# Hybrid encoder trunk on one core: two products of the last FFN's block scheme change places, a step of one unit stands between two of them, and the final sums are spread over three steps

## The chip, the cores and the metric

The kernel runs on one core of a Trainium2 chip. Its time is the device time of one execution in microseconds, from the first to the last instruction and what lies around it; the figure for a kernel is the median of its timed runs.

## The reference

A trunk of two layers (`DEPTH = 2`) over 512 tokens of width 1024. Layer 0 mixes tokens with a gated short convolution, layer 1 with a chunked state-space mixer. Behind each mixer stands a SwiGLU feed-forward network of hidden width 2816. The change is in the second matrix product of the last of these, and in what follows it to the output.

```python
def swiglu_ffn(h, w_in, w_out):
    gate, up = jnp.split(h @ w_in, 2, axis=-1)
    return (jax.nn.silu(gate) * up) @ w_out

# in the loop over layers
        h = rmsnorm(x, norm_g[i, 2]) * (1.0 + scale) + shift
        y = swiglu_ffn(h, f_w_in[i], f_w_out[i])
        x = x + gate * rmsnorm(y, norm_g[i, 3])
    return x
```

Everything is float32. The tensor engine multiplies operands that are split into a high and a low part, so that each product of two tiles is three matmuls (high by high, low by high, high by low).

## The kernel before, in words

**The block scheme.** The last product, `y = hidden @ w2`, has 512 tokens, 2816 hidden values and 1024 columns. The hidden values are taken in pairs of blocks of 128: 11 pairs, numbered p = 0 to 10 (`NP`). Tokens are halved (256 and 256), columns are halved (512 and 512), and the two blocks of a pair are the halves in the third direction. So each pair is a 2 by 2 by 2 block product, done with seven products instead of eight (Strassen's scheme in Winograd's form). The tuple `PRODUCTS` lists the seven: the accumulator that a product adds into (`A`, `B`, `C`, `D`), the weight block (`b11`, `b12`, `b21`, `b22`) and the activation block (`a11`, `a12`, `a21`, `a22`, `s1`). The blocks are overwritten in place with sums as the scheme goes on:

- `t1`: `b12 += b11`, and `t2_`: `b22 += b12`, and `t4`: `b21 += b22`. These are accumulating DMAs, issued on GpSimd's queue (POOL) by `add_`.
- `t3`: `b11 = b22 - b11`, on VectorE (DVE).

In the kernel before, the order is: A with `b11`, B with `b21`, C with `b22` as loaded, A with `b22` after `t2_`, D with `b12` after `t1`, A with `b11` after `t3`, A with `b21` after `t4`. A is one running sum: it is read in between (after its first, second, third product and at the end), while it goes on adding. Each accumulator is two PSUM banks, one for each 128 of the 256 tokens (`t` or `sub` is 0 or 1).

**Units and steps.** The weights of the 11 pairs lie in 9 storage units: pairs (0,1), (2,3), then each of 4 to 10 alone (`units`, `unit_of`). Seven products of 11 pairs are 77 turns; `turns[i]` gives the order of the pairs in product i. Two turns make a step, 39 steps in all (`NT`), the last with one turn. Where a product ends on an odd turn, a step holds the last turn of one product and the first of the next. A step of two turns is 12 matmuls: for `sub` 0, then for `sub` 1, three for each turn (`products`, one recorded line, L1787). The last three steps are run together: `sub` 0 of all three, then `sub` 1.

**Preparation.** `w_prep(n)` splits the weights of step n: ScalarE (ACT) copies the high part (L1752), DVE subtracts for the low part (L1753). `a_prep(n)` does the same for the activations (L1765 and L1766). The split weights have 4 buffers, the split activations 3. So `w_prep(n + 4)` and `a_prep(n + 3)` wait until the tensor engine is through step n.

**The order of the engines' work is written out by hand.** This stretch is under a manual schedule for TensorE, ACT, DVE, POOL and SyncE's queue (SP): each engine takes its instructions in the order in which the code issues them. For each step n the loop issues `products([n])`, then `behind(n)`, then `w_prep(n + 4)`, then `a_prep(n + 3)`; from n = 34 `behind(n)` comes last. `behind(n)` holds what is tied to a step: `t3`, `t2_`, `t4`, and the evacuation of the accumulators into the four quarters of the result (`got["11"]`, `"12"`, `"22"`; the fourth is read from the bank itself), then the sum of squares (`square`, `mean`), the root (`root`), the gate (`gated`, L1991) and the residual with the output's DMA (`x_new`, L1997). L2037 is the subtraction of A from `got["22"]` at n = 32, L2019 that of A from `got["12"]` at n = 21, L2021 the addition of D at n = 27.

SP loads the blocks of `w2` in the order of the `w2_load` calls (L1574); POOL's accumulating DMAs (L1626) wait for those loads and for the splits that still need the old contents.

Of the kernel before, what the change touches and what calls it, by code (L numbers as in the profile page):

```python
# [18 lines left out]
D = 1024  # L19
# [12 lines left out]
MUL, ADD, SUB = ALU.mult, ALU.add, ALU.subtract  # L32
# [3 lines left out]
def trunk_kernel(  # L36
# [9 lines left out]
    act, dve, pe, pool = nc.scalar, nc.vector, nc.tensor, nc.gpsimd  # L46
# [523 lines left out]
    with ExitStack() as ph:  # L570
# [112 lines left out]
        with tc.manual_schedule(engines={PE_ENGINE, mybir.EngineType.SP, mybir.EngineType.Activation,  # L683
# [199 lines left out]
            for p in range(2):  # L883
# [13 lines left out]
            parts = out_begin(0, w_out0, lambda k: acts[k], KD, ggs, xn_tile, "aux", None,  # L897
                              ffn_after(0), ada_tile)
            for k in range(18):
                i, jp = k % 6, 2 + k // 6 * 2  # L900
# [98 lines left out]
        with tc.manual_schedule(engines={PE_ENGINE, mybir.EngineType.SP, mybir.EngineType.Activation,  # L999
# [3 lines left out]
            for i, f in ((0, 0), (2, 0), (1, 1), (3, 1), (4, 2), (5, 3)):  # L1003
# [5 lines left out]
                else:  # L1009
                    gate(f, lead_ps[i])  # L1010
                sums(1)
            parts = out_begin(1, f_w_out[0], lambda k: acts[k], NF, ggs, xn_tile, "aux", ssd_lead,
                              lambda: load_w([(wm_in, P, P)]))
            tiles = []
            for k in range(2 * NF - 6):
# [8 lines left out]
                q, j = divmod(k - 3, 4)  # L1024
# [25 lines left out]
    with ExitStack() as ph:  # L1050
# [299 lines left out]
        def xn_half():  # L1350
            return yp.tile([P, T], F32, tag="y", name="xn")

        parts = out_begin(2, wm_out, y_act, 16, gg2, lambda: (xn_half(), xn_half()), "mm",
                          all_of(ffn_lead(1, tile4b)), ffn_after(1))
# [169 lines left out]
        with tc.manual_schedule(engines={PE_ENGINE}):  # L1524
# [11 lines left out]

    PRODUCTS = (("A", "b11", "a11"), ("B", "b21", "a12"), ("C", "b22", "a12"), ("A", "b22", "a11"),
                ("D", "b12", "s1"), ("A", "b11", "a21"), ("A", "b21", "a22"))  # L1540

    with ExitStack() as ph:
        fo = ph.enter_context(tc.tile_pool(name="fo", bufs=3, reuse_waits="tile"))
# [3 lines left out]
        NP = NF // 2  # L1547
# [5 lines left out]
        units = [(0, 1), (2, 3)] + [(p,) for p in range(4, NP)]  # L1553
# [179 lines left out]

        even = list(range(NP))
        odd = [4, 0, 1, 2, 3] + list(range(5, NP))
        turns = [odd if i % 2 else even for i in range(7)]
        turns[2] = [4, 5, 0, 1, 2, 3] + list(range(6, NP))
        steps = [(i, p) for i in range(7) for p in turns[i]]
        NT = (len(steps) + 1) // 2
        w_of, a_of = {}, {}  # L1740

        def w_prep(n):
            w = whl_p.tile([P, 2, 2, T], F32R, tag="whl", name="whlo")
            part = steps[2 * n:2 * n + 2]
            us = {unit_of[p] for _, p in part}
            if len(us) == 1 and len(part) == 2:
                todo = [(slice(0, 2), b_(us.pop(), PRODUCTS[part[0][0]][1]))]
            else:
                todo = [(slice(q, q + 1), b_(unit_of[p], PRODUCTS[i][1])[:, units[unit_of[p]].index(p):][:, :1])
                        for q, (i, p) in enumerate(part)]  # L1750
            for sl, srcw in todo:
                act.copy(w[:, 0, sl, :], srcw)  # L1752
                dve.tensor_tensor(w[:, 1, sl, :], srcw, w[:, 0, sl, :].bitcast(F32), SUB)  # L1753
            w_of[n] = w

        def a_prep(n):
            a = fo.tile([P, 2, 2, 256], F32R, tag="ao", name="ao")
            part = steps[2 * n:2 * n + 2]
            if len(part) == 2 and part[0][0] == part[1][0] and part[1][1] == part[0][1] + 1:
                todo = [(slice(0, 2), part[0], 2)]  # L1760
            else:
                todo = [(slice(q, q + 1), st, 1) for q, st in enumerate(part)]
            for sl, (i, p), m in todo:
                srca = a_(PRODUCTS[i][2], p, m)
                act.copy(a[:, 0, sl, :], srca)  # L1765
                dve.tensor_tensor(a[:, 1, sl, :], srca, a[:, 0, sl, :].bitcast(F32), SUB)  # L1766
            for _, (i, p), m in todo:
                if i == 0:
                    dve.tensor_tensor(a_("a11", p, m), a_("s1", p, m), a_("a11", p, m), SUB)
                elif i == 1:  # L1770
                    dve.tensor_add(a_("a12", p, m), a_("a12", p, m), a_("a11", p, m))
            a_of[n] = a

        bank = {}

        def products(tiles):
            for sub in range(2):
                for n in tiles:
                    for q, (i, p) in enumerate(steps[2 * n:2 * n + 2]):
                        r = PRODUCTS[i][0]  # L1780
                        if r not in bank:
                            bank[r] = [(mm_ps if r == "C" else aux_ps)(f"c{r}{t}") for t in range(2)]
                        first = i == {"A": 0, "B": 1, "C": 2, "D": 4}[r] and p == turns[i][0]
                        last = p == turns[i][-1]
                        w, a, tk = w_of[n], a_of[n], slice(sub * P, (sub + 1) * P)
                        for k, (hl, al) in enumerate(((0, 0), (1, 0), (0, 1))):
                            pe.matmul(bank[r][sub], a[:, al, q, tk], w[:, hl, q, :],  # L1787
                                      start=first and k == 0, stop=last and k == 2, skip_group_check=True)

        with tc.manual_schedule(engines={PE_ENGINE, mybir.EngineType.SP, mybir.EngineType.Activation,  # L1790
# [5 lines left out]
            def t3(p):  # L1796
                i = unit_of[p]
                q = units[i].index(p)
                dve.tensor_tensor(b_(i, "b11", q), b_(i, "b22", q), b_(i, "b11", q), SUB)

            def t2_(i):
                add_(b_(i, "b22"), b_(i, "b12"))

            def t4(i):
                add_(b_(i, "b21"), b_(i, "b22"))
# [113 lines left out]
            u = UN - 1  # L1919
# [39 lines left out]
            late = range(5, len(units))  # L1959
# [3 lines left out]
            w2_load(4, "b21")  # L1963
            for i in late:
                w2_load(i, "b21")
            for i in (3, 1, 4, *late):
                w2_load(i, "b22", "b12")
            for n in (2, 3):
                w_prep(n)
            a_prep(2)  # L1970
            for i in (2, 3, 0, 1, *range(4, len(units))):
                t1(i)

            st = [{"s2": small(2), "s1": small(1), "b1": small(1)} for _ in range(4)]
# [3 lines left out]
            got = {}  # L1978
# [11 lines left out]
            def gated(src, hf, dst):  # L1990
                dve.tensor_mul(dst, src, gg[hf])  # L1991
                return dst

            def x_new(t, hf, yg, parts=(FULL,), puts=(dma,)):
                for c, put in zip(parts, puts):
                    cx = slice(hf * T + c.start, hf * T + c.stop)
                    dve.scalar_tensor_tensor(xt[t][:, cx], yg[:, c], st[t]["s1"], xt[t][:, cx], MUL, ADD)  # L1997
                    put(out[0, t * P:(t + 1) * P, cx], xt[t][:, cx])

            def behind(n):  # L2000

                if 14 <= n < 14 + NP:
                    t3(turns[5][n - 14])
                for i in (2, 3, 0, 1, *range(4, len(units))):
                    if n == 8 + turns[2].index(units[i][-1]) // 2:
                        t2_(i)
                    if n == 15 + i:
                        t4(i)
                for t in range(2):
                    if n == 5:  # L2010
                        got["11", t] = t2("c11")
                        act.copy(got["11", t], bank["A"][t])
                    elif n == 10:
                        dve.tensor_add(got["11", t], got["11", t], bank["B"][t])
                    elif n == 16:
                        got["12", t] = t2("c12")
                        act.copy(got["12", t], bank["C"][t])
                    elif n == 21:
                        dve.tensor_tensor(got["12", t], got["12", t], bank["A"][t], SUB)  # L2019
                    elif n == 27:  # L2020
                        dve.tensor_add(got["12", t], got["12", t], bank["D"][t])  # L2021
                        got["22", t] = spare[f"c22_{t}"]
                        act.copy(got["22", t], bank["D"][t])
                    elif n in (29, 30):
                        if t == n - 29:
                            square(t, 0, got["11", t])
                            square(t, 1, got["12", t])
                            mean(t)
                    elif n == 31:
                        root(t)  # L2030
                        gated(got["11", t], 0, got["11", t])
                        gated(got["12", t], 1, got["12", t])
                    elif n == 33:
                        x_new(t, 0, got["11", t])
                        x_new(t, 1, got["12", t])
                    elif n == 32:
                        dve.tensor_tensor(got["22", t], got["22", t], bank["A"][t], SUB)  # L2037
                    elif n == 34:
                        square(2 + t, 0, got["22", t])
                        mean(2 + t)  # L2040
                    elif n == 35:
                        gated(got["22", t], 1, got["22", t])

            for n in range(NT - 3):
                products([n])
# [5 lines left out]
                if n + 4 < NT:  # L2051
                    w_prep(n + 4)
                if n + 3 < NT:
                    a_prep(n + 3)
# [42 lines left out]
```

## Time and profile before

| | us |
|---|---|
| median of three runs | 1351.39 (1349.91 to 1351.97) |
| the profiled execution's own time | 1351.48 |
| its span, first to last instruction | 1349.2 |
| TensorE busy in the span | 1329.8 (99%) |
| VectorE busy | 984.9 (73%) |
| ScalarE busy | 618.2 (46%) |
| first matmul of the changed product, from the span's start | 1226.38 |

The profile is of one execution. Times in its views are counted from the start of the span. PE is TensorE's matmuls, PEld its weight loads, DVE VectorE, ACT ScalarE, POOL GpSimd, SP SyncE. A row of the timeline is: start, length, engine, line, operation, tiles written and read, shape, count, and in brackets how long the engine was idle before it and what ended that. Matmuls overlap, so a row's length runs some 0.16 us past the start of what follows it. PEclk is the share of the full clock that TensorE was granted.

### The profile page before, as it was taken

To read this page: it belongs to the slowest core of one execution; us is meant where nothing else is said; L and a number is where in the kernel's file an instruction comes from. 1 tells how busy PE (TensorE), PEld (TensorE's weight loads), DVE (VectorE), ACT (ScalarE), POOL (GpSimd) and SP (SyncE) were. 2 spreads that over 40 slices of the span, in tenths; PEclk is the share of its full clock that TensorE was granted. 3 is DMA by queue.
4 is the path that set the end of the run, shared out by engine and by line. 5 is a ranking of instruction groups with operands and counts; after the bars stand their busy time and mean duration, and the time that the engine had idled before them with its cause. 6 is when DMAs were issued, how large, how long until landed. Compare 5 with 4: busy or idle time off the path is not lost.

```text
span 1349.2 us, 19124 instructions
## 1 busy us (share of the span) xinstructions
PE 1329.8 (99%) x7485; PEld 1145.6 (85%) x7485; DVE 984.9 (73%) x1581; ACT 618.2 (46%) x995; POOL 65.1 (5%) x82
## 2 busy tenths in 40 slices
PE   8999999999999999999999999999999999999896
PEld 6788889888888888898888888888899999998685
DVE  5588866778777322668988988887678777758696
ACT  5323355222322212655554555554474555545564
POOL 0000000000000000000000000000000111200420
PEclk9999999999999999999999999999999999999998
DMA  9757760777776322414534243413342888868851
GB/s 307 237 180 230 253 203 1 233 249 233 236 250 203 125 94 91 132 33 144 157 110 138 80 127 110 140 65 123 113 122 61 219 198 213 215 198 268 142 105 63
DMA packets 199886, 215.90 MB, mean 160 GB/s; under 512 B 8292, under 2 KB 148468, under 8 KB 198772
## 3 DMA queue, kind: packets, MB, share of 16 engines
q1 hardware_dynamic: 186384, 184.74, 44.1%
q0 software_dynamic: 9264, 17.04, 7.3%
q10 hardware_dynamic: 4148, 12.90, 3.1%
q8 instruction: 59, 0.97, 0.3%
q14 instruction: 31, 0.25, 0.1%
HBM read 195.37 MB, written 2.24 MB: 146 GB/s over the span
## 4 chain that ended last, share of the span: by engine, by line
PE 89%; DMA 4%; DVE 2%; ACT 2%; issue 2%; SPq 1%; POOL 1%; DVEq 0%; POOLq 0%; ACTq 0%
PE ip L276 14%; PE ip L278 14%; PE ip L277 14%; PE sA L1694 6%; PE y L378 6%; PE y L379 6%; PE y L380 6%; PE sC L1694 3%; PE cA L1787 2%; PE li L276 2%; PE li L278 2%; PE li L277 2%; PE li L756 2%; PE sB L1694 1%; PE yd L1283 1%
## 5 line engine op out<-in xcount | busy, mean ns | idle before, releaser
L276 PE MATMUL ip<-h,whl 128*128 128x512 f32 x840 | 331.2, 394 | 0.2 <-DVE cv L863 0.2
L278 PE MATMUL ip<-h,whl 128*128 128x512 f32 x840 | 327.2, 390 | 0.0
L277 PE MATMUL ip<-h,whl 128*128 128x512 f32 x840 | 327.0, 389 | 0.0
L276 PEld LDWEIGHTS ip<-h,whl 128*128 128x128 f32 x840 | 157.7, 188 | 33.9 <-issue 1.8
L278 PEld LDWEIGHTS ip<-h,whl 128*128 128x128 f32 x840 | 157.6, 188 | 33.2
L277 PEld LDWEIGHTS ip<-h,whl 128*128 128x128 f32 x840 | 157.8, 188 | 31.8
L222 DVE TENSOR_TENSOR whl<-wst,whl 128x1024 fp32r<-128x1024 f32 x99 | 120.4, 1221 | 60.6 <-ACT whl L221 60.4
L124 DVE SCALAR_TENSOR_TENSOR ada_acc<-ada_st,csil,ada_acc 128x512 f32<-128x512 f32 x140 | 105.0, 750 | 3.9 <-DMA ada_st<-in_ada_w_dram 0.4
L204 DVE TENSOR_TENSOR whlo<-wsto,whlo 128x1024 fp32r<-128x1024 f32 x41 | 49.9, 1224 | 78.1 <-ACT whlo L203 78.0
L221 ACT CAST whl<-wst 128x1024 fp32r<-128x1024 f32 x99 | 103.0, 1041 | 4.3 <-DMA wst<-in_a_w_in_dram 2.2
L276 PE MATMUL li<-h,whl 128*128 128x256 f32 x288 | 83.2, 289 | 0.0
L278 PE MATMUL li<-h,whl 128*128 128x256 f32 x288 | 81.6, 283 | 0.0
L277 PE MATMUL li<-h,whl 128*128 128x256 f32 x288 | 81.5, 283 | 0.0
L203 ACT CAST whlo<-wsto 128x1024 fp32r<-128x1024 f32 x41 | 42.6, 1050 | 76.3 <-PE y L380 71.1
L1694 PE MATMUL sA<-tq,whl 128*128 128x256 f32 x576 | 74.6, 283 | 0.3 <-DVE g L1720 0.3
L1694 PEld LDWEIGHTS sA<-tq,whl 128*128 128x128 f32 x576 | 71.6, 192 | 0.6 <-DVE g L1720 0.5
L1787 PE MATMUL cA<-whlo,ao 128*128 128x512 f32 x264 | 64.3, 402 | 6.0 <-DVE w2h L2037 3.7
L378 PE MATMUL y<-whlo,ff 128*128 128x512 f32 x176 | 68.6, 390 | 0.0
L380 PE MATMUL y<-whlo,ff 128*128 128x512 f32 x176 | 68.5, 389 | 0.0
L379 PE MATMUL y<-whlo,ff 128*128 128x512 f32 x176 | 68.5, 389 | 0.0
L1787 PEld LDWEIGHTS cA<-whlo,ao 128*128 128x128 f32 x264 | 51.3, 195 | 18.0 <-issue 4.1
L1142 DVE SCALAR_TENSOR_TENSOR cu<-ip,cols,cu 128x511 f32<-128x511 f32 (+2 forms) x84 | 62.8, 748 | 3.9 <-ACT cu L1139 1.4
(328 smaller groups left out, 2436.9 us busy)
## 6 DMA issues: line engine op xcount, KB each, us to landing
ada_st<-in_ada_w_dram SPq DMA_DIRECT2D x96, 512.0 KB, 5.3
wst<-in_f_w_in_dram SPq DMA_DIRECT2D x26, 1024.0 KB, 6.5
wst<-in_m_w_in_dram SPq DMA_DIRECT2D x14, 1024.0 KB, 5.4
wsto<-in_f_w_out_dram SPq DMA_DIRECT2D x10, 1024.0 KB, 5.0
wst<-in_m_w_in_dram SPq DMA_DIRECT2D x20, 512.0 KB, 5.1
wst<-in_a_w_in_dram SPq DMA_DIRECT2D x9, 1024.0 KB, 6.1
wsu<-in_f_w_in_dram SPq DMA_DIRECT2D x17, 512.0 KB, 5.9
csb<-cs_d ACTq DMA_DIRECT2D x8, 1024.0 KB, 5.1
```

The costliest lines, as they stand in the source:

```text
L124: dve.scalar_tensor_tensor(acc, w, csil[:, k:k + 1], acc, MUL, ADD)
L221: later.append((lambda sw=sw, w=w: act.copy(w[:, 0, :nk, :], sw), lambda sw=sw, w=w: dve.tensor_tensor(w[:, 1, :nk, :], sw, w[:, 0, :nk, : ...
L222: lambda sw=sw, w=w: dve.tensor_tensor(w[:, 1, :nk, :], sw, w[:, 0, :nk, :].bitcast(F32), SUB)))
L276: pe.matmul(dst, w_at(w, 0, kk), a[:, 0, sl], start=start, stop=False)
L277: pe.matmul(dst, w_at(w, 0, kk), a[:, 1, sl], start=False, stop=False)
L278: pe.matmul(dst, w_at(w, 1, kk), a[:, 0, sl], start=False, stop=stop)
L378: pe.matmul(pst, a[:, 0, tk], wt[:, 0, kk, :], start=k == 0, stop=False)
L379: pe.matmul(pst, a[:, 0, tk], wt[:, 1, kk, :], start=False, stop=False)
L380: pe.matmul(pst, a[:, 1, tk], wt[:, 0, kk, :], start=False, stop=k == K - 1)
L1142: dve.scalar_tensor_tensor(u[:, sft:], pst[:, :T - sft], w[3 - sft], u[:, sft:], MUL, ADD)
L1694: pe.matmul(dst, w[:, wl, k0 + k, :], moving(q, k, al), skip_group_check=True, start=q in ("P1", "P5", "P2") and k == 0 and i == 0, stop=k ...
L1787: pe.matmul(bank[r][sub], a[:, al, q, tk], w[:, hl, q, :], start=first and k == 0, stop=last and k == 2, skip_group_check=True)
```

## The change

The fourth and the fifth product change places: D with `b12` comes before A with `b22`. The pairs' order becomes the plain one in every product but the second and the fourth. The turns are paired in three runs: products 0 to 4 (55 turns, 28 steps, the last with one turn), product 5 (6 steps, the last with one turn) and product 6 (the same). That is 40 steps: step 27 is the last turn of product 4 alone, step 33 the last turn of product 5 alone, step 39 that of product 6.

The order of the last loads changes: unit 1 before units 3 and 4. `t1` goes 0, 2, 1, 3, ... instead of 2, 3, 0, 1, .... `t2_` follows the plain order, `t4` starts at step 19 instead of 15, and `t3` stands at steps 17 to 27, at the end of `behind`, instead of 14 to 24 at its start. D is added to `got["12"]` and copied at n = 21, A is subtracted from `got["12"]` at n = 27 and from `got["22"]` at n = 33. The root moves from n = 31 to 34. The gates and residuals of the first 256 tokens, which stood at n = 31 and 33, stand at 34, 35 and 36: the left columns' gate at 34 and residual at 35, the right columns' at 35 and 36. The squares of `got["22"]` move from n = 34 to 35 and its gate from 35 to 36.

```diff
-    PRODUCTS = (("A", "b11", "a11"), ("B", "b21", "a12"), ("C", "b22", "a12"), ("A", "b22", "a11"),
-                ("D", "b12", "s1"), ("A", "b11", "a21"), ("A", "b21", "a22"))
+    PRODUCTS = (("A", "b11", "a11"), ("B", "b21", "a12"), ("C", "b22", "a12"), ("D", "b12", "s1"),
+                ("A", "b22", "a11"), ("A", "b11", "a21"), ("A", "b21", "a22"))
...
-        turns = [odd if i % 2 else even for i in range(7)]
-        turns[2] = [4, 5, 0, 1, 2, 3] + list(range(6, NP))
-        steps = [(i, p) for i in range(7) for p in turns[i]]
-        NT = (len(steps) + 1) // 2
+        turns = [odd if i in (1, 3) else even for i in range(7)]
+        parts = []
+        for run in ((0, 1, 2, 3, 4), (5,), (6,)):
+            steps = [(i, p) for i in run for p in turns[i]]
+            parts += [steps[k:k + 2] for k in range(0, len(steps), 2)]
+        NT = len(parts)
...
-            for i in (3, 1, 4, *late):
+            for i in (1, 3, 4, *late):
                 w2_load(i, "b22", "b12")
...
-            for i in (2, 3, 0, 1, *range(4, len(units))):
+            for i in (0, 2, 1, *range(3, len(units))):
                 t1(i)
...
-                if 14 <= n < 14 + NP:
-                    t3(turns[5][n - 14])
-                for i in (2, 3, 0, 1, *range(4, len(units))):
-                    if n == 8 + turns[2].index(units[i][-1]) // 2:
-                        t2_(i)
-                    if n == 15 + i:
-                        t4(i)
...
                     elif n == 21:
-                        dve.tensor_tensor(got["12", t], got["12", t], bank["A"][t], SUB)
-                    elif n == 27:
                         dve.tensor_add(got["12", t], got["12", t], bank["D"][t])
                         got["22", t] = spare[f"c22_{t}"]
                         act.copy(got["22", t], bank["D"][t])
+                    elif n == 27:
+                        dve.tensor_tensor(got["12", t], got["12", t], bank["A"][t], SUB)
+                    elif n == 33:
+                        dve.tensor_tensor(got["22", t], got["22", t], bank["A"][t], SUB)
...
-                    elif n == 31:
+                    elif n == 34:
                         root(t)
                         gated(got["11", t], 0, got["11", t])
-                        gated(got["12", t], 1, got["12", t])
-                    elif n == 33:
-                        x_new(t, 0, got["11", t])
-                        x_new(t, 1, got["12", t])
-                    elif n == 32:
-                        dve.tensor_tensor(got["22", t], got["22", t], bank["A"][t], SUB)
-                    elif n == 34:
+                    elif n == 35:
                         square(2 + t, 0, got["22", t])
                         mean(2 + t)
-                    elif n == 35:
+                        gated(got["12", t], 1, got["12", t])
+                        x_new(t, 0, got["11", t])
+                    elif n == 36:
                         gated(got["22", t], 1, got["22", t])
+                        x_new(t, 1, got["12", t])
+                for i, u in enumerate(units):
+                    if n == 8 + u[-1] // 2:
+                        t2_(i)
+                    if n == 19 + i:
+                        t4(i)
+                if 17 <= n < 17 + NP:
+                    t3(turns[5][n - 17])
```

More of the change, by code (lines that the diff above doesn't have):

```diff
@@ L1743, in w_prep @@
             w = whl_p.tile([P, 2, 2, T], F32R, tag="whl", name="whlo")
-            part = steps[2 * n:2 * n + 2]
+            part = parts[n]
             us = {unit_of[p] for _, p in part}
@@ L1757, in a_prep @@
             a = fo.tile([P, 2, 2, 256], F32R, tag="ao", name="ao")
-            part = steps[2 * n:2 * n + 2]
+            part = parts[n]
             if len(part) == 2 and part[0][0] == part[1][0] and part[1][1] == part[0][1] + 1:
@@ L1778, in products @@
                 for n in tiles:
-                    for q, (i, p) in enumerate(steps[2 * n:2 * n + 2]):
+                    for q, (i, p) in enumerate(parts[n]):
                         r = PRODUCTS[i][0]
@@ L1782, in products @@
                             bank[r] = [(mm_ps if r == "C" else aux_ps)(f"c{r}{t}") for t in range(2)]
-                        first = i == {"A": 0, "B": 1, "C": 2, "D": 4}[r] and p == turns[i][0]
+                        first = i == {"A": 0, "B": 1, "C": 2, "D": 3}[r] and p == turns[i][0]
                         last = p == turns[i][-1]
```

## Prediction

> **What bounds the kernel now.** I read the page first: TensorE (PE) is busy for nearly the whole span, so the time can move only where PE stands still or runs slowly. The page's costliest groups name one line of the changed product.
>
> ```profile
> PE 1329.8 (99%) x7485; PEld 1145.6 (85%) x7485; DVE 984.9 (73%) x1581; ACT 618.2 (46%) x995; POOL 65.1 (5%) x82
> L1787 PE MATMUL cA<-whlo,ao 128*128 128x512 f32 x264 | 64.3, 402 | 6.0 <-DVE w2h L2037 3.7 <-ACT ao L1765 1.7 <-DVE ao L1766 0.6
> ```
>
> PE's timeline then shows where the waits lie and lets me count. (Three rows of three matmuls each are left out between 1272.22 and 1276.52.)
>
> ```profile
> 1226.38 14.44 PE L1787 MATMUL cA<-whlo,ao 128*128 128x512 f32 x63
> ...
> 1256.30 13.76 PE L1787 MATMUL cC<-whlo,ao 128*128 128x512 f32 x60
> 1270.93 0.73 PE L1787 MATMUL cC<-whlo,ao 128*128 128x512 f32 x2 [0.87 <-ACT ao L1765]
> 1272.22 0.50 PE L1787 MATMUL cC<-whlo,ao 128*128 128x512 f32 x1 [0.55 <-DVE ao L1766]
> ...
> 1276.52 0.73 PE L1787 MATMUL cA<-whlo,ao 128*128 128x512 f32 x2 [1.73 <-ACT ao L1765]
> 1277.86 13.45 PE L1787 MATMUL cA<-whlo,ao 128*128 128x512 f32 x58 [0.61 <-DVE ao L1766]
> 1291.14 14.44 PE L1787 MATMUL cD<-whlo,ao 128*128 128x512 f32 x63
> ...
> 1306.78 14.44 PE L1787 MATMUL cA<-whlo,ao 128*128 128x512 f32 x63
> 1324.92 17.84 PE L1787 MATMUL cA<-whlo,ao 128*128 128x512 f32 x66 [3.70 <-DVE w2h L2037]
> ```
>
> The 63 matmuls from 1291.14 are followed 14.28 us later by the next row (left out), so one takes 14.28 / 63 = 0.2267 us, a step of two turns 2.72, a step of one turn 1.36; the last matmul of a row shows 0.16 beyond that. The 462 matmuls should take 104.73 + 0.16 = 104.89 us. They take from 1226.38 to 1324.92 + 17.84 = 1342.76, which is 116.38. The 11.49 too many lie in three lumps (11.50 by their rounding):
>
> - steps 16 to 18: the 60 matmuls from 1256.30 are over at 1269.90; from there to 1277.86 are 7.96 us for 14 matmuls (3.17), and 58 more end 0.13 short of 1291.14: **4.92**;
> - the handover from step 32 to 33: 1306.78 + 14.28 = 1321.06 to 1324.92: **3.86**;
> - the last 66 matmuls take 17.84 instead of 15.12: **2.72**, with no wait shown.
>
> The windows view (us; busy time of PE, PEld, DVE, ACT, POOL; PEclk; DMA) tells what the third lump is.
>
> ```profile
> 1269.00:1279.00 10.00, 6.24 (x24) 3.92 (x23) 5.52 (x9) 5.76 (x11) 5.04 (x6) 1.00 0.72 122
> 1323.00:1324.00 1.00, 0.00 (x0) 0.00 (x0) 1.00 (x2) 0.01 (x1) 0.00 (x0) 0.81 0.00 0
> 1324.00:1330.00 6.00, 5.08 (x12) 4.09 (x13) 5.83 (x10) 0.00 (x0) 0.00 (x0) 0.50 0.22 81
> ```
>
> The granted clock fell to half. A mean of 0.81 over one microsecond is 0.38 us at half, so it fell at 1323.62, 2.40 us after PE's last matmul ended (1306.78 + 14.44 = 1321.22), and 6 us later it was still at half. Through the waits of 0.87, 0.55, 1.73 and 0.61 in 1269 to 1279 it stayed at 1.00. So the long wait of 3.86 costs 6.58 with its slow matmuls.
>
> **Lump one: the chain of accumulating DMAs.** ACT's two waits ahead of the stalled steps, and POOL's rows, show the cause.
>
> ```profile
> 1269.53 1.05 ACT L1752 CAST whlo<-w2t 128x1024 fp32r<-128x1024 f32 x1 [4.89 <-DMA w2t<-w2t]
> 1274.90 1.04 ACT L1752 CAST whlo<-w2t 128x1024 fp32r<-128x1024 f32 x1 [3.71 <-DMA w2t<-w2t]
> 1236.79 0.88 POOL L1626 DMA_DIRECT2D w2s<-w2s  x1 [25.40 <-DMA w2t<-in_f_w_out_dram]
> 1263.81 1.22 POOL L1626 DMA_DIRECT2D w2t<-w2t  x1 [2.25 <-DVE whlo L1753]
> 1269.79 1.20 POOL L1626 DMA_DIRECT2D w2t<-w2t  x1 [4.76 <-issue]
> ```
>
> The fourth product needs `b22 + b12`. Its `t2_` of units 0 and 1 goes out at 1263.81 and 1269.79, because the raw `b22` must first be split for product C, and the splits wait for 5.7 us (1263.81 to 1269.53) and 5.1 us (1269.79 to 1274.90) of transfer. After the change product D stands there, which needs only `b12 + b11`, a `t1`. `t1` waits for loads and for no product. In before, `t1` of unit 3 held the queue until 1236.79 with that of unit 0 behind it; now units 0 and 2, loaded early, go ahead, and unit 1 is loaded before unit 3. D's first split comes behind step 12, at 1226.38 + 13 x 2.72 = 1261.7, those of units 0 and 1 at 1264.5 and 1267.2, some 25 us past 1236.79. `t2_` is next needed behind step 18, at 1278.1; unit 0's can start behind the split in step 7 (1248.1 and some 2.5 for it) and takes the same 5.7. Even if it starts as late as in before it lands at 1269.5, unit 1's at 1274.9, ahead of 1278.1 and 1280.8. `t3` sits on `t2_` too and moves with it, from step 14 to 17; `t4` has from step 19 to the splits behind step 30. The gate's two broadcasts on SP, still at n = 26, wait for `b12` to be read, which now comes earlier. So lump one goes: **-4.92**. Bounds: 0 if POOL's queue is as late for D, and -4.92; I take the whole, since D has the margin just shown.
>
> **Lump two becomes two handovers.** PE may write bank A of half 0 again only when DVE has read it. In before, D stands between one reading (n = 21) and A's next use, so only n = 32 is exposed. After the change A follows A at 27/28 and at 33/34. How long is each? In before DVE came late for a reason of its own:
>
> ```profile
> 1318.13 1.28 ACT L1987 ACT_TABLE_LOAD   x1
> ...
> 1319.75 0.17 DVE L1988 RECIPROCAL ss<-ss 128x1 f32<-128x1 f32 x1 [0.30 <-ACT ss L1987]
> 1319.83 1.27 DVE L1991 TENSOR_TENSOR c<-c,w2h 128x512 f32<-128x512 f32 x2
> 1321.03 0.15 DVE L1988 RECIPROCAL ss<-ss 128x1 f32<-128x1 f32 x1
> 1321.10 1.27 DVE L1991 TENSOR_TENSOR c<-c,w2h 128x512 f32<-128x512 f32 x2
> ...
> 1324.09 1.28 DVE L2037 TENSOR_TENSOR w2h<-w2h,cA 128x512 f32<-128x512 f32 x2
> ```
>
> The root's table load held ACT, and four gates held DVE until 1322.3, ahead of the splits and of the reading at 1324.09. PE went on 0.83 after that start. The change takes root and gates away from there. What stays ahead of the reading is `w_prep` and `a_prep` of the step before. Step 26 of before has exactly that order, with the same two half tiles, and D's reading in the place of A's:
>
> ```profile
> 1304.94 1.14 ACT L1752 CAST whlo<-w2s 128x512 fp32r<-128x512 f32 x2 [1.15 <-PE cD L1787]
> 1305.99 0.62 ACT L1765 CAST ao<-raw 128x512 fp32r<-128x512 f32 x1
> 1305.60 1.30 DVE L1753 TENSOR_TENSOR whlo<-w2s,whlo 128x512 fp32r<-128x512 f32 x2 [0.46 <-ACT whlo L1752]
> 1306.81 0.68 DVE L1766 TENSOR_TENSOR ao<-raw,ao 128x512 fp32r<-128x512 f32 x1
> 1307.41 1.27 DVE L2021 TENSOR_TENSOR c<-c,cD 128x512 f32<-128x512 f32 x2
> ```
>
> Step 26 ended at 1291.14 + 5 x 2.72 = 1304.74. The reading starts 2.67 later, PE could go on 0.83 after that, 3.50 past the step's end. The single step takes 1.36 of it: 2.14 are left, and I take **2.18** for each handover, as one `t3`, an operation of the size of the 0.68 above, crowds the first by a few hundredths. PE's second half waits for DVE's second reading (0.6 later), which step 28's first half (1.36) covers. Two handovers: **+4.36** in place of 3.86. Bounds for each: 0.15 if DVE were free at once (0.83 less the 0.68 of the single step's other half), and 3.86 as in before. The row of step 26 is much the nearest.
>
> Behind the waiting subtraction on DVE stand `w_prep(31)` and `a_prep(30)` (1.9 us together by the rows above); `a_prep(30)` is needed two steps, 5.4 us, after PE goes on, and they are through by then. At n = 21 DVE gets D's addition, ACT the copies and DVE a `t3`; in before the same stood at n = 27 and no matmul waited in the 63 from 1306.78, and the `t3` falls into DVE's wait for ACT. The squares at n = 29 and 30 stay and load ACT as before.
>
> **Lump three.** PE would be idle for some 2.18 - 0.16 = 2.02 us, between the 1.73 that left the clock alone and the 2.40 after which it fell. I take no fall: **-2.72**. The Trainium skill, "TensorE: Matmul & The Clock Gate" (Part 1: The HAM clock gate), says that the clock falls to half after an idle window of about 3.4 us; this trace shows the fall after 2.40 us of idling, so the rule is too mild here. By the rule both handovers would be safe and the sum is as below.
>
> **The end.** The moved gates and residuals now stand at n = 34 to 36. Count DVE from the end of step 34. ACT casts until 1.89 (0.20 + 1.05 + 0.64), table load to reciprocal is 1.62 (1318.13 to 1319.75), so DVE starts the roots and two gates at 3.51 and is done at 4.87 (two reciprocals 0.16, two gates 1.20). Splits for steps 39 and 38 (two of 0.6): 6.07. Two means, two gates, two residuals (0.1 as a reciprocal, 0.6, and 0.67, the 0.75 of the row below less the 0.08 by which DVE's rows overlap): 8.81. Only then comes the low half of step 39's activations.
>
> ```profile
> 1336.44 0.42 DVE L1766 TENSOR_TENSOR ao<-raw,ao 128x256 fp32r<-128x256 f32 x1 [0.45 <-ACT ao L1765]
> ...
> 1340.98 0.75 DVE L1997 SCALAR_TENSOR_TENSOR x<-yg,ss,x 128x512 f32<-128x512 f32 x1
> ...
> 1343.52 0.69 DVE L1991 TENSOR_TENSOR yg<-cA,w2h 128x512 f32<-128x512 f32 x1 [1.13 <-ACT w2s L1981]
> ```
>
> It is ready at about 9.26, and PE wants it for the third matmul of step 39, at 5.44 + 2.72 + 0.45 = 8.61: **+0.65** (0 to 1.5). The rest (two gates, two residuals, 2.54) and the third quarter's three operations end at about 13.8. PE's last matmul ends at 9.26 + 16 x 0.2267 + 0.16 = 13.05, and the last gate follows it by 0.76 (1342.76 to 1343.52), at 13.8: just covered, 0 to 0.5. From there to the end the instructions are the same.
>
> **Sum.** -4.92 + 4.36 - 3.86 - 2.72 + 0.65 = -6.49. The profiled execution took 1351.48 (span 1349.2), 0.09 over the median of 1351.39. 1351.48 - 6.49 = **1345.0**, span 1342.7.
>
> **The rivals.**
>
> - The clock falls after one handover, chance 0.20. For: 2.02 lies nearer to 2.40 than to nothing. Price as in before, 2.72: 1347.7. After both (0.05): 1350.4.
> - POOL's chain is as late for D as for `t2_`, so the exchange does not do its work, 0.07: lump one stays, 1349.9. Against: the margin above.
> - The end: DVE's queue from n = 34 on costs 1 to 2 us more or nothing (0.10): 1344.3 to 1347.
> - Slower: the second handover of A onto A (27/28) is what the old order had avoided by putting D there. If DVE reaches each reading as late as at n = 32 before (3.86), the clock falls twice; with half of 6.8 us lost each time the two cost 2 x (3.86 + 3.4) = 14.5, with the end 15.2, against 11.5: 1355.2. With 2.72 each it is 1353.8. It decides from 5.4 us for each handover. Against: root and gates no longer stand there. Chance 0.06.
>
> **How the numbers follow.** The forecast itself has 0.52. The range takes it with its bounds (both handovers half a microsecond shorter and nothing lost at the end, 1.65 less: 1343.3), the one fall of the clock and the end: 1343.2 to 1348.6, which holds 0.82. A measurement of this kernel can tell about 0.2%, 2.7 us, from no change, so faster means below 1348.7: 0.52 + 0.20 + 0.10 = 0.82. Same: 0.05 + 0.07, and slower 0.06.
>
> **What would show it.** Right: no PE wait at steps 16 to 18 and no ACT wait for an accumulating DMA at L1754; two PE waits of about 2.0 us behind DVE's subtractions L2018 and L2020; PEclk 1.00 throughout; a short PE wait on the activations' split in the last step; 66 matmuls less slow at the end. Wrong: a granted clock of 0.50 after a handover, a handover over 3 us, or D's splits waiting for DMA.

## The result, and the profile after

| | before | after |
|---|---|---|
| median of five runs, us | 1351.39 (1349.68 to 1352.04) | 1345.17 (1344.72 to 1345.47) |
| ratio to before | | 0.9957, 95% interval 0.9942 to 0.9971 |
| the profiled execution's own time, us | 1351.48 | 1345.17 |
| its span, us | 1349.2 | 1343.0 |

The changed kernel is faster by 6.2 us; the forecast was 6.4. The line numbers below are those of the changed kernel: L1789 is the matmuls (L1787 before), L1754 and L1755 the weights' split, L1767 and L1768 the activations' split, L2018 and L2020 the two readings of A.

PE's timeline after, from product C on:

```profile
1256.34 14.44 PE L1789 MATMUL cC<-whlo,ao 128*128 128x512 f32 x63
1270.62 0.84 PE L1789 MATMUL cD<-whlo,ao 128*128 128x512 f32 x3
1271.30 0.84 PE L1789 MATMUL cC<-whlo,ao 128*128 128x512 f32 x3
1271.98 14.44 PE L1789 MATMUL cD<-whlo,ao 128*128 128x512 f32 x63
1286.26 15.12 PE L1789 MATMUL cA<-whlo,ao 128*128 128x512 f32 x66
1303.40 15.22 PE L1789 MATMUL cA<-whlo,ao 128*128 128x512 f32 x66 [2.02 <-ACT ao L1767]
1320.60 11.61 PE L1789 MATMUL cA<-whlo,ao 128*128 128x512 f32 x50 [1.97 <-ACT ao L1767]
1332.60 3.92 PE L1789 MATMUL cA<-whlo,ao 128*128 128x512 f32 x16 [0.39 <-DVE ao L1768]
```

The row of C runs straight into D's: no bracket until 1303.40. Three waits are left, where the forecast put them. With 0.2267 us for a matmul they cost 2.18 (66 matmuls from 1286.26 are through at 1301.22), 2.24 (1318.36 to 1320.60) and 0.67 (1331.93 to 1332.60), and the last 16 take 0.13 too long: 5.22 in all, where before had 11.49 and the forecast 5.01.

The windows around the three waits (us; busy time of PE, PEld, DVE, ACT, POOL; PEclk; DMA) show the clock.

```profile
1299.00:1310.00 11.00, 8.98 (x40) 7.16 (x39) 9.22 (x16) 6.76 (x15) 0.00 (x0) 1.00 0.00 1
1315.00:1331.00 16.00, 14.03 (x62) 11.29 (x62) 12.68 (x24) 10.48 (x21) 0.00 (x0) 1.00 0.01 1
```

PEclk is 1.00 in both, so the 2.72 us of slow matmuls are gone in this execution.

The brackets at 1303.40 and 1320.60 name ACT's L1767, whose row ended last. DVE's timeline shows the reading that PE waited for:

```profile
1300.77 0.68 DVE L1755 TENSOR_TENSOR whlo<-w2t,whlo 128x512 fp32r<-128x512 f32 x1
1301.37 0.68 DVE L1755 TENSOR_TENSOR whlo<-w2s,whlo 128x512 fp32r<-128x512 f32 x1
1301.97 0.68 DVE L1768 TENSOR_TENSOR ao<-raw,ao 128x512 fp32r<-128x512 f32 x1
1302.58 1.28 DVE L2018 TENSOR_TENSOR c<-c,cA 128x512 f32<-128x512 f32 x2
```

Splits of step 30's weights and step 29's activations, then the reading, then PE 0.82 us after the reading's start: the order and the distance that the prediction took from step 26 of before. The same distance, 0.82 to 0.84, stands in every handover with a wait in the profiles below, and in several of them the bracket itself names DVE's reading.

### The profile page after: what moved, and what is told of

Its sections match the earlier page's. It is cut to its first block, busy times and chain, and to the rows that moved or that the text cites. A ratio compares the mean times of both kernels' runs of the same rounds, so it can differ in the third digit from the quotient of the medians.

```text
span 1343.0 us, 19136 instructions
## 1 busy us (share of the span) xinstructions
PE 1326.6 (99%) x7485; PEld 1143.8 (85%) x7485; DVE 985.2 (73%) x1581; ACT 618.2 (46%) x995; POOL 65.3 (5%) x82
## 3 DMA queue, kind: packets, MB, share of 16 engines
HBM read 195.37 MB, written 2.24 MB: 147 GB/s over the span
## 4 chain that ended last, share of the span: by engine, by line
PE 91%; issue 3%; DMA 2%; ACT 2%; DVE 1%; SPq 0%; DVEq 0%; ACTq 0%; POOLq 0%
PE ip L276 14%; PE ip L278 14%; PE ip L277 14%; PE sA L1694 6%; PE y L378 6%; PE y L380 6%; PE y L379 6%; PE cA L1789 4%; PE sC L1694 3%; PE li L756 2%; PE li L276 2%; PE li L277 2%; PE li L278 2%; PE sB L1694 2%; PE yd L1283 1%
## 5 line engine op out<-in xcount | busy, mean ns | idle before, releaser
L1789 PE MATMUL cA<-whlo,ao 128*128 128x512 f32 x264 | 61.2, 390 | 4.4 <-ACT ao L1767 4.0
L1789 PEld LDWEIGHTS cA<-whlo,ao 128*128 128x128 f32 x264 | 49.3, 188 | 15.7 <-ACT ao L1767 4.8
```

Of the source, the lines that this page charges most:

```text
L1789: pe.matmul(bank[r][sub], a[:, al, q, tk], w[:, hl, q, :], start=first and k == 0, stop=last and k == 2, skip_group_check=True)
```

## The experiments

Each has its edit (lines left out are marked ...), the expectation on record and the result. Ratios are to the kernel before on the same chip, with 95% intervals.

### The sums moved alone, in the old order of products

At n = 32 of the kernel before:

```diff
-                    elif n == 31:
-                        root(t)
-                        gated(got["11", t], 0, got["11", t])
-                        gated(got["12", t], 1, got["12", t])
-                    elif n == 33:
-                        x_new(t, 0, got["11", t])
-                        x_new(t, 1, got["12", t])
                     elif n == 32:
                         dve.tensor_tensor(got["22", t], got["22", t], bank["A"][t], SUB)
+                        if t == 1:
+                            for s in range(2):
+                                root(s)
+                                gated(got["11", s], 0, got["11", s])
+                                gated(got["12", s], 1, got["12", s])
                     elif n == 34:
...
+                        x_new(t, 0, got["11", t])
+                        x_new(t, 1, got["12", t])
```

> The kernel before with one thing changed: at n = 32 the subtraction of A from got22 comes first and the root and the four gates behind it (they stood at n = 31), and the four residuals move from n = 33 to 34. Products keep their old order. My theory (three separate lumps): the wait at steps 16 to 18 stays (4.9 us), the handover at 32/33 shrinks from 3.86 to about 0.8, because step 32 has two turns and covers 2.72 of the 3.50 us, and the granted clock stays at 1.00, which saves 2.72 more: 5.8 us less, 1345.6. Rival (the exchange of the two products is what brings the gain, the place of the sums is worth nothing): 1351.4.

Measured: 1347.37 (1345.51 to 1349.03), ratio 0.9968 (0.9956 to 0.9980). The profiled execution took 1345.51. Its PE timeline:

```profile
1306.37 14.44 PE L1787 MATMUL cA<-whlo,ao 128*128 128x512 f32 x63
1321.59 15.21 PE L1787 MATMUL cA<-whlo,ao 128*128 128x512 f32 x66 [0.78 <-ACT ss L1987]
```

The handover is 0.94 (1320.65 to 1321.59; DVE's reading starts at 1320.76, 0.83 before PE goes on), the 66 matmuls behind it run at full speed, and that execution came out 0.1 from the 1345.6 expected. The rival's 1351.4 is out: the place of the sums has its own worth. But the median lies 1.8 above my figure. The timed executions list 0.999 as granted clock for the one of 1345.51, 0.998 for those of 1345.99 to 1348.07 and 0.996 for that of 1349.03: that suggests a fall of the clock that the first profile did not have. The same kernel was profiled once more, on another chip.

> The same kernel as the run with the sums moved alone, profiled once more. Its first profile had the clock at 1.00 throughout and took 1345.5, its timed executions up to 1349.0 with lower granted clocks. My theory: in most executions the waits at steps 16 to 18 (1.74 and 0.61 within 3 us) let the clock fall there, 1.6 us for each fall: 1347 to 1349 with PEclk 0.50 for 3.4 us near 1277. Rival (the spread comes from elsewhere, such as the loads at the start): clock 1.00 through the stretch and another time.

Measured: 1347.86 in this one execution, granted clock 0.998. PE's timeline and the clock behind the waits at steps 16 to 18:

```profile
1271.10 0.73 PE L1787 MATMUL cC<-whlo,ao 128*128 128x512 f32 x2 [1.22 <-ACT ao L1765]
...
1276.69 0.74 PE L1787 MATMUL cA<-whlo,ao 128*128 128x512 f32 x2 [1.74 <-ACT ao L1765]
1278.03 15.05 PE L1787 MATMUL cA<-whlo,ao 128*128 128x512 f32 x58 [0.61 <-DVE ao L1766]
...
1323.78 15.21 PE L1787 MATMUL cA<-whlo,ao 128*128 128x512 f32 x66 [0.78 <-ACT ss L1987]
```
```profile
1278.00:1280.00 2.00, 1.97 (x7) 1.55 (x8) 2.00 (x4) 1.68 (x4) 0.86 (x1) 0.75 1.04 175
1280.00:1281.00 1.00, 1.00 (x4) 0.81 (x3) 1.00 (x3) 0.81 (x2) 0.00 (x0) 0.50 1.13 188
```

The waits of 1.74 and 0.61 are those of before, and here the clock fell behind them: 58 matmuls took 15.05 us where before took 13.45, 1.60 more. So the first lump can have a second price that before's profile did not show, since there PEclk stayed at 1.00 through 1269 to 1279. The clock is not all that differs from the first profile of this kernel, though. The first wait of the lump, 1.22 here, was 0.30 there (0.87 in before):

```profile
1270.52 0.73 PE L1787 MATMUL cC<-whlo,ao 128*128 128x512 f32 x2 [0.30 <-ACT ao L1765]
```

The 2.35 us between the two executions are thus the clock's 1.6 and the wait's 0.9, to within 0.2.

### Root and gates back ahead of the second reading

In the changed kernel, `root(t)` and both `gated` of the first 256 tokens go from n = 34 and 35 to n = 32:

```diff
-                    elif n == 34:
+                    elif n == 32:
                         root(t)
                         gated(got["11", t], 0, got["11", t])
+                        gated(got["12", t], 1, got["12", t])
                     elif n == 35:
...
-                        gated(got["12", t], 1, got["12", t])
```

> The changed kernel with root and all four gates of the first 256 tokens put back to one step ahead of the second reading of A (n = 32, as n = 31 stood to n = 32 before). My theory: the splits of step 36 and the reading come behind the table load and the gates, PE waits at 33/34 for about 4.6 us instead of 2.2, the granted clock falls to half after it and costs 2.7 to 3.4; some 0.7 comes back at the end, where less is left on VectorE: 1349.5 to 1350.6. The handover at 27/28 keeps its 2.0 and its clock of 1.00. Rival (the root's place is worth nothing): 1345.2.

Measured: 1349.76 (1348.16 to 1351.25), ratio 0.9985 (0.9976 to 0.9994). PE's timeline and clock, in the execution of 1348.16:

```profile
1303.23 15.24 PE L1789 MATMUL cA<-whlo,ao 128*128 128x512 f32 x66 [2.02 <-ACT ao L1767]
1322.81 16.81 PE L1789 MATMUL cA<-whlo,ao 128*128 128x512 f32 x66 [4.34 <-DVE w2h L2020]
```
```profile
1323.00:1324.00 1.00, 1.00 (x5) 0.78 (x5) 1.00 (x3) 0.00 (x0) 0.00 (x0) 0.80 0.00 0
1324.00:1327.00 3.00, 3.00 (x9) 2.32 (x8) 1.07 (x2) 0.00 (x0) 0.00 (x0) 0.50 0.00 0
```

The first handover kept its 2.02, the second went to 4.34 and the clock fell, at 1.6 us (16.81 against 15.24 for 66 matmuls). Taking root and gates away from there is what makes the second handover short. The median lies in the range expected, but partly by luck: the profiled execution is the fastest of the ten, below the range, as one fall cost 1.6 and not 2.7 to 3.4. The other nine took 1.0 to 3.1 us more and list granted clocks of 0.996 and 0.997 against its 0.998; where their clock fell further no profile shows.

### The old order of loads and `t1`

```diff
-            for i in (1, 3, 4, *late):
+            for i in (3, 1, 4, *late):
...
-            for i in (0, 2, 1, *range(3, len(units))):
+            for i in (2, 3, 0, 1, *range(4, len(units))):
                 t1(i)
```

> The changed kernel with the loads of b22 and b12 in the old order (units 3, 1, 4) and t1 in the old order (units 2, 3, 0, 1). My theory: with D in the fourth place there are over 20 us of margin, the order is worth nothing: 1345.2 within 0.5, no PE wait at steps 16 to 18. Rival (it was the earlier loads and t1 that took the wait away): up to 4.9 more, 1350.

Measured: 1345.53 (1344.54 to 1346.30), ratio 0.9950 (0.9934 to 0.9967). No PE wait at steps 16 to 18 is among PE's waits in the product (us in total, times, longest):

```profile
PE cA L1789 <- ACT ao L1767: 4.0, 2, 2.0
PE cA L1789 <- DVE ao L1768: 0.4, 1, 0.4
```

The exchange of products, with the `t2_`, `t3` and `t4` that move with it, removes the first lump; the new order of loads and `t1` adds nothing that shows. The profiled execution, of 1346.30, had a fall of the clock at the first handover:

```profile
1303.20 16.84 PE L1789 MATMUL cA<-whlo,ao 128*128 128x512 f32 x66 [2.02 <-ACT ao L1767]
```
```profile
1304.00:1305.00 1.00, 1.00 (x5) 0.77 (x4) 1.00 (x3) 0.00 (x0) 0.00 (x0) 0.63 0.01 0
1305.00:1307.00 2.00, 2.00 (x6) 1.63 (x5) 1.06 (x2) 0.00 (x0) 0.00 (x0) 0.50 0.00 0
1307.00:1308.00 1.00, 1.00 (x4) 0.78 (x4) 0.00 (x0) 0.22 (x1) 0.00 (x0) 0.66 0.00 0
```

A mean of 0.63 in the first microsecond puts the fall at 1304.26, one of 0.66 in the last puts its end at 1307.68: 3.42 us, 1.62 us lost (16.84 against 15.22). This is the prediction's first rival, at a lower price than it was given.

### The two waits made longer

One operation more on DVE ahead of each reading, its result unused:

```diff
                     elif n == 27:
+                        if t == 0:
+                            dve.tensor_add(spare["junk"], got["11", 0], got["11", 1])
                         dve.tensor_tensor(got["12", t], got["12", t], bank["A"][t], SUB)
                     elif n == 33:
+                        if t == 0:
+                            dve.tensor_add(spare["junk"], got["11", 0], got["11", 1])
```

> The changed kernel with one more VectorE operation over 128x512 (0.6 us, its result unused) ahead of each of the two readings of A. It lengthens both waits of PE from 2.0 to 2.6. My theory (the clock falls where PE idles for about 2 us or more inside one window of 3.41 us): 1.2 from the waits, and in more than half of the executions one fall of the clock to half for 3.4 us, 1.6 more: median 1347 to 1348.2, with the granted clock of the slower executions lower. Rival (a fall needs an idle window of some 3.4 us, so waits of 2.6 are safe): 1346.4, all executions at the same granted clock.

Measured: 1348.02 (1346.27 to 1349.29 in ten runs), ratio 0.9977 (0.9968 to 0.9986). The one of 1346.27 lists 0.999 as granted clock, the others 0.996 to 0.998. The waits alone (2.62 and 2.57 in that profile, 0.6 each more) give the 1346.3. The other nine lie in two groups, five from 1347.51 to 1348.07 and four from 1349.07 to 1349.29, some 1.5 and 2.9 us above it. One fall cost 1.6 us in the profiles above, so by estimate these are one fall and two. That the rest is the clock rests on these times and the listed clocks; none of the nine was profiled. The rival's equal clocks are out: waits of 2.6 us are not safe.

### The step of one turn in the middle

```diff
-            parts += [steps[k:k + 2] for k in range(0, len(steps), 2)]
+            one = len(steps) - (1 if run == (6,) else 7)
+            parts += [steps[k:k + 2] for k in range(0, one, 2)] + [steps[one:one + 1]]
+            parts += [steps[k:k + 2] for k in range(one + 1, len(steps), 2)]
```

> The changed kernel with the step of one turn moved from the end of product 4 and of product 5 to the middle (pair 4 alone), so that the last step ahead of each reading of A has two turns. My theory: the reading starts 2.67 us after the end of the step before, whatever the last step's length, and PE goes on 0.83 later; a last step of 2.72 covers 2.72 of the 3.50 instead of 1.36, so both waits fall from 2.0 to some 0.6 in the waits view: 2.8 us less, 1342.4. Rival (the wait is the path from the last matmul through VectorE back to PE, which a longer step does not shorten): 1345.2.

Measured: 1342.91 (1342.31 to 1343.55), ratio 0.9933 (0.9919 to 0.9948). PE's waits in the product, in the same form:

```profile
PE cA L1791 <- DVE w2h L2022: 0.9, 1, 0.9
PE cA L1791 <- DVE c L2020: 0.6, 1, 0.6
PE cA L1791 <- DVE ao L1770: 0.4, 1, 0.4
```

0.6 and 0.9 in place of 2.0 and 2.0: the last step's length covers DVE's queue, as reckoned. The second is 0.25 longer than I had it.

### The reading ahead of the splits, alone and with the step in the middle

Here the changed kernel issues the next step's products early, so that DVE takes the reading before `w_prep` and `a_prep` of the step before:

```diff
...
             for n in range(NT - 3):
-                products([n])
+                if n not in (27, 33):
+                    products([n])
                 if n < 34:
                     behind(n)
+                if n in (26, 32):
+                    products([n + 1])
+                    read("12" if n == 26 else "22")
```

> The changed kernel with the two readings of A by VectorE (n = 27 and 33) issued ahead of the splits of the step before (those of steps 30 and 36 of the weights, 29 and 35 of the activations) instead of behind them. My theory (the handover is as long as what stands ahead of the reading in VectorE's queue): the reading starts when the single step's first half is done, 0.9 us after the step before, PE goes on 0.83 later, 1.7, of which the step covers 1.36; PE waits 0.2 to 0.4 instead of 2.0 at each handover, 3.4 less: 1341.8; the splits that are pushed back by 1.2 are still in time. Rival (the pushed splits become the next wait, as in a queue that is full anyway): 1344 to 1345 with waits on the activations' split at steps 29 and 35.

Measured: 1341.60 (1341.35 to 1341.78), ratio 0.9928 (0.9913 to 0.9943). PE's rows:

```profile
1301.58 15.22 PE L1789 MATMUL cA<-whlo,ao 128*128 128x512 f32 x66 [0.22 <-DVE c L2043]
1317.00 11.61 PE L1789 MATMUL cA<-whlo,ao 128*128 128x512 f32 x50 [0.19 <-DVE w2h L2043]
1329.00 3.92 PE L1789 MATMUL cA<-whlo,ao 128*128 128x512 f32 x16 [0.39 <-DVE ao L1768]
```

What stands ahead of the reading in DVE's queue was nearly the whole handover. The pushed splits were in time.

> The step of one turn in the middle (as in the run with the single step inside) and the early reading together. My theory: the reading of the first half is over before the last step of two turns ends, so no wait is left at either handover: 4.4 less than the changed kernel, 1340.8, or up to 0.4 more where the split for step 29 comes late. Rival (the two edits mend the same thing, so the second adds nothing): as the better of the two alone.

Measured: 1340.76 (1340.54 to 1340.88), ratio 0.9922 (0.9907 to 0.9936). No wait is left at the handovers:

```profile
1286.51 41.41 PE L1791 MATMUL cA<-whlo,ao 128*128 128x512 f32 x182
1328.32 3.92 PE L1791 MATMUL cA<-whlo,ao 128*128 128x512 f32 x16 [0.39 <-DVE ao L1770]
```

### The end

With both edits, root and four gates at n = 33 behind the splits, the left residuals at 34, the right at 35:

```diff
...
+                if n == 33:
+                    for t in range(2):
+                        root(t)
+                        gated(got["11", t], 0, got["11", t])
+                        gated(got["12", t], 1, got["12", t])
                 if n >= 34:
                     behind(n)
```

> As the run with single step inside and early reading, and root with all four gates of the first 256 tokens at n = 33 behind the splits, where VectorE and ScalarE idle; residuals at n = 34 and 35. My theory: the low half of the last step's activations is in time, the wait of 0.4 to 0.7 in the last step goes: 1340.1. Rival (the end is bound by VectorE's queue behind the last matmul, not by that split): as the run without it, 1340.8.

Measured: 1341.76 (1341.65 to 1342.00), ratio 0.9929 (0.9913 to 0.9946): 1.0 slower than without it, against my 0.7 faster. PE's and DVE's timelines show what I had left out:

```profile
1327.46 5.71 PE L1791 MATMUL cA<-whlo,ao 128*128 128x512 f32 x22 [0.86 <-DVE ss L1988]
...
1324.79 1.41 DVE L2001 SCALAR_TENSOR_TENSOR x<-c,ss,x 128x512 f32<-128x512 f32 x2
1326.12 0.69 DVE L1757 TENSOR_TENSOR whlo<-w2h,whlo 128x512 fp32r<-128x512 f32 x1
1326.72 0.69 DVE L1770 TENSOR_TENSOR ao<-raw,ao 128x512 fp32r<-128x512 f32 x1
```

The two residuals now stand ahead of the split for step 38, which ends at 1327.41, and PE waited 0.86 for it (the bracket names DVE's next row). So they went one step later again (`x_new` left at 35, right at 36):

> As the run with the end changed too, but the residuals one step later again (left columns at n = 35, right columns at n = 36, both behind the splits of their step), since two residuals ahead of the split for step 38 had made PE wait 0.86 there. Gates stay at n = 33. My theory: the splits for steps 38 and 39 are both in time, no wait of PE is left from step 0 to 39, and VectorE is through by the last gate: 0.4 less than the run with single step inside and early reading alone, 1340.4. Rival (VectorE's queue of the last steps only moves its work from one wait to another): 1340.8 or more, with a new wait.

Measured: 1340.60 (1340.42 to 1340.80), ratio 0.9924 (0.9907 to 0.9940), no different from 1340.76. PE's timeline and the windows:

```profile
1286.12 45.72 PE L1791 MATMUL cA<-whlo,ao 128*128 128x512 f32 x198
```
```profile
1320.00:1324.00 4.00, 4.00 (x20) 3.30 (x19) 4.00 (x9) 3.55 (x8) 0.00 (x0) 1.00 0.00 0
1324.00:1328.00 4.00, 3.88 (x17) 2.61 (x15) 4.00 (x10) 0.61 (x3) 0.00 (x0) 1.00 0.09 33
1328.00:1331.00 3.00, 3.00 (x14) 2.47 (x15) 3.00 (x6) 0.98 (x3) 0.00 (x0) 1.00 0.60 223
```

No wait of any length is listed, yet 198 matmuls take 45.72 where 45.05 are due: the 0.67 is still lost, in small pieces. The time lies between my 1340.4 and the rival's 1340.8 and does not tell them apart. DVE is busy for every one of the 11 us from 1320 on, which agrees with the rival: the end is bound by DVE's queue, and a new order only moves the wait. That no order could save the 0.67 is not shown. This version and the one with the two edits alone beat both kernels: the changed one by some 4.5 us, the one before by 0.8%.

## Why the prediction was right

By its own steps, for the profiled execution:

| step | forecast | measured |
|---|---|---|
| waits at steps 16 to 18 | -4.92 | -4.92: none left |
| two handovers | +4.36 - 3.86 | +4.42 - 3.86 |
| slow clock | -2.72 | -2.72 |
| the end | +0.65 | +0.80 |
| sum | -6.49 | -6.27 (11.49 to 5.22) |

**The chain of DMAs.** Right, with margin to spare. POOL's rows after:

```profile
1237.60 1.20 POOL L1626 DMA_DIRECT2D w2t<-w2t  x1 [22.41 <-PE cA L1789]
...
1255.95 1.20 POOL L1626 DMA_DIRECT2D w2t<-w2t  x1 [2.16 <-DVE whlo L1755]
1261.35 2.14 POOL L1626 DMA_DIRECT2D w2t<-w2t  x2 [4.20 <-DVE whlo L1755]
```

`t1` of unit 1 goes out at 1237.60 instead of 1248.47, `t2_` of units 0 and 1 at 1255.95 and 1261.35, and the latter are first needed at 1278. Unit 0's could start later than reckoned (1255.95 for 1250.6): its split was over at 1250.7, but POOL was still issuing `t1` until 1252.93. The bound, 1263.81 as in before, covered that. ACT's L1754 waits for no DMA in the product. In the run with the old order of loads `t1` of unit 1 went out at 1248.16, `t2_` of units 0 and 1 at 1260.13 and 1265.52, and no wait came of it either: it is the exchange that gives the margin.

**The handovers.** Step 26 of before was the right pattern: 2.14 to 2.18 forecast, 2.18 and 2.24 measured, the same on both sides, since DVE's queue ahead of the reading is the same but for one `t3`. Four runs move the wait as this reading says: 2.0 to 4.3 with root and gates ahead, 2.0 to 2.6 with an operation more ahead, 0.6 and 0.9 with a longer last step, 0.2 with the reading ahead of the splits.

**The clock.** The forecast took no fall at 2.02 us of idling and gave a fall 1 chance in 5. The five runs of the changed kernel all list 0.999. But the nearly equal kernel with the old loads had a fall at the same wait of 2.02, so the chance was real, and that none of the five had one is in part luck. The price was too high: 1.62, not 2.72, since the half clock lasted 3.42 us there. In before it lasted twice that, 6.82 (from 1323.62 to 1330.44):

```profile
1330.00:1331.00 1.00, 1.00 (x4) 0.79 (x4) 0.00 (x0) 0.58 (x2) 0.00 (x0) 0.78 1.03 381
```

The length of the wait is not the reason, since the run with the root ahead waited 4.34 and lost only 1.57. What differs in before is that PE was still idle for the first 1.30 us at half clock. Nor does the length of a wait tell when the clock falls, as the forecast took it: with the old loads, with the root ahead and in the second profile of the sums moved alone PE had already gone on for 0.8 to 1.1 us. The forecast also left out that the first lump can let the clock fall (seen once, in the run with the sums moved alone); its removal is worth more than 4.92 there. That fits the spread of before's times, 2.4 us in its five runs against 0.8 for the changed kernel; it was not shown run by run, and the lump's own waits vary too.

**The end.** 0.67 and 0.13 for 0.65. The low half of the last step's activations was ready 9.22 us after the end of step 34 (1320.60 + 2.72 to 1332.54), where the forecast had 9.26:

```profile
1332.13 0.41 DVE L1768 TENSOR_TENSOR ao<-raw,ao 128x256 fp32r<-128x256 f32 x1
```

The last gate, at 1337.28, follows PE's end (1336.52) by 0.76 as before, so DVE was just through, as reckoned.

## What to carry to other kernels

When an accumulator is read and written on, count what stands ahead of the reading in the reader's queue, and what the tensor engine still has to do in that time: a longer last step or a reading issued earlier hides it, and a root or a gate in front of it makes it long. A wait of the tensor engine of some 2 us can have a second price in the clock, and several short waits within a few microseconds can bring it as one long one does. When a moved operation saves nothing, look whether the engine it sits on is already busy throughout.

## What the runs showed of the hardware

A wait of 2.0 us was enough for the granted clock to fall to half in one execution (old order of loads) and not in others (the changed kernel, the first handover with the root ahead). Waits of 1.74 and 0.61 with two matmuls between them were enough in one profile of the run with the sums moved alone and not in the other. The three falls that came when PE was already running again lasted 3.4 us and cost 1.6 us each. In the 3.4 us before the four falls PE had stood still for some 2.0 (old loads), 1.7 (sums alone), 2.6 (root ahead) and 2.4 us (before), an estimate from the rows and PEclk above: half of that stretch or more each time, and never the whole. The Trainium skill, "TensorE: Matmul & The Clock Gate" (Part 1: The HAM clock gate), has a free-running window of 3.4 us and a fall after an idle window. The stretch of 3.42 us at half clock agrees; the fall after 2.0 us of idling, and after shorter waits with matmuls between, does not agree with an idle window. What share of a window decides was not settled by these runs.
